# Windowed-softmax heads taken by fours in a decoder layer, with the probabilities turned by DMA

## The chip, the core and the metric

The kernel runs on one core of one Trainium2 chip. The core has TensorE (PE, matrix products, with weight loads PEld beside them), VectorE (DVE), ScalarE (ACT), GpSimd (POOL) and SyncE (SP), which here only issues DMAs. The metric is the time of one execution in microseconds; the median of three runs is compared. Lower is better.

## The reference

One decoder layer on 256 positions of width 2048, in float32, batch 1:

```python
mod = (silu(c) @ w_ada + b_ada).reshape(9, D)                 # conditioning: shifts, scales, gates
x = x + 0.5 * mod[2] * swiglu(modulate(rms_norm(x), mod[0], mod[1]), w_ffn1_gu, w_ffn1_down)
h = modulate(rms_norm(x), mod[3], mod[4])
rq, rk, rv, rg, sq, sk, sv, gl_ret, gl_swa = split(h @ w_in)  # one projection, 2048 x 13312
y_ret = (silu(rg) * group_rms(retention(rotary(rq), rotary(rk), rv))) @ w_ret_branch
y_swa = swa_with_sinks(sq, sk, sv, sinks) @ w_swa_branch
x = x + mod[5] * ((sigmoid(gl_ret) * y_ret + sigmoid(gl_swa) * y_swa) @ w_out)
x = x + 0.5 * mod[8] * swiglu(modulate(rms_norm(x), mod[6], mod[7]), w_ffn2_gu, w_ffn2_down)
return rms_norm(x)
```

The part that the change is about is `swa_with_sinks`: 32 query heads of 64 share 8 key and value heads (four each). Positions stand in two blocks of 128. A query of the first block sees keys of its own block, one of the second sees both, within a window of 128. Each head has a learned "sink" logit that joins the softmax's sum and takes no value.

## The kernel before

Nearly all work is projections. A weight tile `raw` of 4 x 128 rows by 512 columns comes by DMA (`load`, L328), is split in two halves of 1024 columns each: ACT casts a half to `wh` (L351), DVE subtracts to get the remainder `wl` (L353), in three buffers each. PE multiplies each half with both blocks of 128 positions: 12 products of 128x512, L343 (high times high), L344 (low activations), L345 (low weights). `in_chunk` makes 512 columns of the combined projection: four such tiles, so eight halves.

Other work is hung between the tiles. After each half `tick()` may advance the conditioning, `ada_pass`, a multiply-and-sum on DVE over rows of `w_ada` (L206) that share the pool of four `raw` buffers; `pace["rate"]` is the number of passes per half. After each tile `turn_step()` advances transpositions by DMA (`turn_by_dma`: ACT writes a tile's low and high 16-bit halves as two planes, SP issues a transposing DMA at L500, ACT puts the planes together at L511), and `step()` advances a list of side work, `side`: the windowed softmax, then the retention heads. Except on SP, whose order is the program's, a scheduler then orders each engine's instructions; each engine runs its own list in order.

The windowed softmax goes by pairs of heads, 16 pairs. `window_weights(pair)`: logits on PE, two heads beside each other in the array's two row halves (L1097 for the first block of queries, L1101 for the second), scaled and masked by DVE (L1105), maxima, sum and sink on DVE, four exponentials on ACT (L1136), four scalings on DVE (L1145). `window_values(pair)`, a step later: six turns of 128x128 on PE against the identity (`transpose_to`, L478), evacuated by ACT (L479), then the products with the values (L1165, L1170) and a copy into `qo` (L1177). The residual `x` stays in SBUF in `x_sb` all the while. The table `dec` of decay factors for retention is loaded by POOL when the combined projection begins.

Of the kernel before, what the change touches and what calls it, by code (L numbers as in the profile page):

```python
# [17 lines left out]
P = 128  # L18
# [59 lines left out]
def layer_kernel(  # L78
# [257 lines left out]
    def products(banks, ah, al, wh, wl, starts, ends, halves=range(NT)):  # L336
        n = ah.shape[1]
        for j in range(n):
            first, last = starts and j == 0, ends and j == n - 1
            for t in halves:  # L340
                ts = slice(t * P, (t + 1) * P)
                ps = banks[t]
                nc.tensor.matmul(ps, ah[:, j, ts], wh[:, j, :], start=first, stop=False)  # L343
                nc.tensor.matmul(ps, al[:, j, ts], wh[:, j, :], start=False, stop=False)  # L344
                nc.tensor.matmul(ps, ah[:, j, ts], wl[:, j, :], start=False, stop=last)  # L345

    def split(pool, tag, src, n, hi_engine="act"):
        k = src.shape[1]
        hi = pool.tile([P, 2, n], F32R, tag=tag + "h", name=nm(tag + "h"))[:, :k, :]
        lo = pool.tile([P, 2, n], F32R, tag=tag + "l", name=nm(tag + "l"))[:, :k, :]  # L350
        cast.append(nc.scalar.copy(hi, src).ins)  # L351
        del cast[:-1]
        nc.vector.tensor_sub(lo, src, hi.bitcast(F32))  # L353
        return hi, lo

    cast = []

    def pair_tile():
        return asp.tile([P, 2, CH], F32, tag="a", name=nm("a"))
# [725 lines left out]

    mask = small_c[:, C_MASK : C_MASK + 3 * P]

    def window_weights(pair):

        kv = pair // 2  # L1090
        lg = pair_tile()[:, :, : 3 * P]

        both = [side_bank() for _ in range(2)]
        halves = [slice(i * HD, (i + 1) * HD) for i in range(2)]
        with tc.high_priority(offset=300):
            for ps, hs in zip(both, halves):
                nc.tensor.matmul(  # L1097
                    ps[:, :P], qo[hs, pair, :P], skt[hs, kv, :P], start=True, stop=True
                )
            for ps, hs in zip(both, halves):  # L1100
                nc.tensor.matmul(  # L1101
                    ps[:, P : 3 * P], qo[hs, pair, P:], skt[hs, kv, :], start=True, stop=True
                )
        for i, ps in enumerate(both):
            nc.vector.scalar_tensor_tensor(  # L1105
                out=lg[:, i, :],
                in0=ps[:, : 3 * P],
                scalar=HD**-0.5,
                in1=mask,
                op0=ALU.mult,  # L1110
                op1=ALU.add,
            )
        mx = small(4, "mx")
        m2 = mx.rearrange("p (t i) -> p t i", t=2)
        nc.vector.tensor_reduce(out=m2[:, 0, :], in_=lg[:, :, :P], axis=AX.X, op=ALU.max)
        nc.vector.tensor_reduce(out=m2[:, 1, :], in_=lg[:, :, P:], axis=AX.X, op=ALU.max)
        sb = sink_b[:, 2 * pair : 2 * pair + 2]
        nc.vector.tensor_tensor(
            out=m2, in0=m2, in1=sb[:, None, :].broadcast_to([P, 2, 2]), op=ALU.max
        )  # L1120
        ng = small(4, "ng")
        nc.vector.tensor_scalar(out=ng, in0=mx, scalar1=-1.0, scalar2=None, op0=ALU.mult)
        se = small(4, "se")
        nc.vector.tensor_tensor(
            out=se.rearrange("p (t i) -> p t i", t=2),
            in0=ng.rearrange("p (t i) -> p t i", t=2),
            in1=sb[:, None, :].broadcast_to([P, 2, 2]),
            op=ALU.add,
        )
        nc.scalar.activation(se, se, AF.Exp)  # L1130
        sm = small(4, "sm")
        for t in range(2):
            for i in range(2):
                seg = lg[:, i, :P] if t == 0 else lg[:, i, P:]
                z = 2 * t + i
                nc.scalar.activation(  # L1136
                    seg, seg, AF.Exp, bias=ng[:, z : z + 1], accum_out=sm[:, z : z + 1]
                )
        nc.vector.tensor_add(sm, sm, se)
        nc.vector.reciprocal(sm, sm)  # L1140
        for t in range(2):
            for i in range(2):
                seg = lg[:, i, :P] if t == 0 else lg[:, i, P:]
                z = 2 * t + i
                nc.vector.tensor_scalar(  # L1145
                    out=seg, in0=seg, scalar1=sm[:, z : z + 1], scalar2=None, op0=ALU.mult
                )
        return lg

    def window_values(pair, lg):  # L1150

        kv = pair // 2
        prs = []
        for i in range(2):
            pr = a512()
            transpose_to(
                pr[:, : 3 * P], lambda j: lg[:, i, j * P : (j + 1) * P], 3, bank()
            )
            prs.append(pr)
        po = bank()  # L1160
        vs = slice(kv * HD, (kv + 1) * HD)
        halves = [slice(i * HD, (i + 1) * HD) for i in range(2)]
        with tc.high_priority(offset=300):
            for hs, pr in list(zip(halves, prs))[::-1]:
                nc.tensor.matmul(  # L1165
                    po[hs, :P], sv[:, 0, vs], pr[:, :P], start=True, stop=True
                )
            for t in range(2):
                for hs, pr in list(zip(halves, prs))[::-1]:
                    nc.tensor.matmul(  # L1170
                        po[hs, P:S],
                        sv[:, t, vs],
                        pr[:, (t + 1) * P : (t + 2) * P],
                        start=t == 0,
                        stop=t == 1,
                    )
        nc.any.tensor_copy(qo[:, pair, :], po[:, :S])  # L1177

    before = []

    def window(pair):
        lg = window_weights(pair)
        yield
        if before:
            window_values(*before.pop())
        before.append((pair, lg))
        if pair == QH // 2 - 1:
            yield
            window_values(*before.pop())
        yield  # L1190

    for ci in range(4):
        b = in_chunk(O_SQ + ci * CH)
        work = []
        for t in range(NT):
            u = t512()
            nc.any.tensor_copy(u, b[t])
            work.append(turn_by_dma(qo[:, ci * 4 : ci * 4 + 4, t * P : (t + 1) * P], u))
        pairs = range(ci * 4, ci * 4 + 4)
        soon(later(work, lambda pairs=pairs: side.extend(window(pair) for pair in pairs)))  # L1200


    qk = slot().rearrange("p (a h s) -> p a h s", a=2, h=RH)
# [34 lines left out]
    def retention(h):  # L1238
# [9 lines left out]
        dh = dec[:, h * S : (h + 1) * S]  # L1248
# [67 lines left out]
    for p in range(2):  # L1316
# [125 lines left out]
```

## Time and profile before

| | |
|---|---|
| runs | 2400.08, 2400.95, 2401.19 us; median 2400.95 |
| profiled execution | 2398.28 us, span 2396.5 us |
| granted TensorE clock | 0.999 |
| busy time of the span | PE 99%, PEld 81%, DVE 71%, ACT 54% |
| windowed softmax on PE | from 880.0 us (first logits) to 1113.8 us (last values) |
| DMA | 615.31 MB, mean 257 GB/s |

The page is one profiled execution. A row of a group gives the line, the engine, the tiles (out<-in) and sizes, the count, then busy time in us and the mean in ns, then the idle time before them and what ended it. Matmuls are pipelined, so one that lasts 0.39 us by its row may follow the last after 0.23. The timeline's first column is the start, the second the length, both in us.

### The profile page before, as it was taken

The numbers are of one execution on the slowest core, as the hardware profiler recorded it, in microseconds if no ns is written. First come the engines' busy times: TensorE is split into PE (matmuls) and PEld (weight loads), VectorE is DVE, ScalarE is ACT, GpSimd is POOL, SyncE is SP. The second block draws the span as 40 slices with busy tenths as digits, with TensorE's granted clock in tenths as the row PEclk, the third lists the DMA queues.
The fourth block names the chain that finished last, engine by engine and source line by source line (L and its number), as shares of the span: only waits on it lengthen the run. The fifth ranks groups of instructions, "written<-read, shape, count | busy, mean of one in ns | idle before, by whom it ended". The sixth has DMA issues, their size and how long they took to land. (4 is left out here: it accounts for less than half of the span.)

```text
span 2396.5 us, 28841 instructions
## 1 busy us (share of the span) xinstructions
PE 2365.2 (99%) x10662; PEld 1937.3 (81%) x10662; DVE 1696.6 (71%) x2707; ACT 1302.2 (54%) x1807; POOL 5.6 (0%) x14
## 2 busy tenths in 40 slices
PE   7999999999999999999999999999999999999998
PEld 5788888888788887778888888887888888888886
DVE  6987799788977667876666776767655555545656
ACT  6554456454456566665556554466445445454544
POOL 0000000000000000000000000000000000000000
PEclk9999999999999999999999999999999999999999
DMA  9978789998875888765679887765777777765563
GB/s 357 365 280 273 267 294 336 345 335 329 315 250 211 272 262 244 231 213 202 236 256 288 265 270 276 268 203 193 230 243 237 247 253 241 259 220 190 182 205 126
DMA packets 309614, 615.31 MB, mean 257 GB/s; under 512 B 75169, under 2 KB 75553, under 8 KB 290657
## 3 DMA queue, kind: packets, MB, share of 16 engines
q1 hardware_dynamic: 307970, 606.82, 74.6%
q0 software_dynamic: 928, 5.61, 0.6%
q8 instruction: 83, 1.36, 0.2%
q10 hardware_dynamic: 576, 1.05, 0.1%
q14 instruction: 57, 0.47, 0.1%
HBM read 595.06 MB, written 2.12 MB: 249 GB/s over the span
## 5 line engine op out<-in xcount | busy, mean ns | idle before, releaser
L353 DVE TENSOR_TENSOR wl<-raw,wh 128x1024 fp32r<-128x1024 f32 x794 | 967.2, 1224 | 553.0 <-ACT wh L351 548.8
L351 ACT CAST wh<-raw 128x1024 fp32r<-128x1024 f32 x794 | 835.1, 1053 | 932.3 <-PE pa L344 903.2
L343 PE MATMUL pa<-wh,hh 128*128 128x512 f32 x2192 | 856.2, 392 | 2.9 <-ACT wh L351 2.9
L344 PE MATMUL pa<-wh,hl 128*128 128x512 f32 x2192 | 855.7, 391 | 0.3 <-DVE hl L600 0.3
L345 PE MATMUL pa<-wl,hh 128*128 128x512 f32 x2192 | 783.6, 391 | 1.1 <-DVE wl L353 0.9
L343 PEld LDWEIGHTS pa<-wh,hh 128*128 128x128 f32 x2192 | 411.8, 188 | 89.6 <-ACT wh L351 4.4
L344 PEld LDWEIGHTS pa<-wh,hl 128*128 128x128 f32 x2192 | 412.0, 188 | 88.3 <-issue 3.0
L345 PEld LDWEIGHTS pa<-wl,hh 128*128 128x128 f32 x2192 | 409.6, 188 | 89.2 <-DVE wl L353 2.8
L344 PE MATMUL pa<-wh,a 128*128 128x512 f32 x944 | 365.2, 389 | 0.0
L343 PE MATMUL pa<-wh,a 128*128 128x512 f32 x944 | 349.8, 390 | 1.8 <-DVE t L606 1.4
L345 PE MATMUL pa<-wl,a 128*128 128x512 f32 x944 | 348.9, 390 | 1.4 <-DVE wl L353 1.4
L206 DVE CUSTOM_DVE_ANT_0 raw<-raw,cact 128x512 f32<-128x512 f32 (+1 forms) x296 | 189.9, 696 | 46.8 <-DMA raw<-in_w_ada_dram 40.0
L343 PEld LDWEIGHTS pa<-wh,a 128*128 128x128 f32 x944 | 177.3, 188 | 40.0 <-DVE t L606 2.2
L345 PEld LDWEIGHTS pa<-wl,a 128*128 128x128 f32 x944 | 177.0, 188 | 39.6 <-DVE wl L353 3.0
L344 PEld LDWEIGHTS pa<-wh,a 128*128 128x128 f32 x944 | 177.2, 188 | 36.5 <-DVE a L386 0.2
L206 DVE CUSTOM_DVE_ANT_0 slot<-slot,cact 128x512 f32<-128x512 f32 (+1 forms) x216 | 170.2, 838 | 8.6 <-DMA slot<-in_w_ada_dram 8.6
L511 ACT COPY slot<-back 128x512 uint16<-128x512 uint16 x124 | 82.7, 766 | 0.0
L386 DVE TENSOR_TENSOR a<-slot,a 128x512 fp32r<-128x512 f32 x118 | 80.9, 687 | 1.3 <-ACT a L385 1.3
L385 ACT CAST a<-slot 128x512 fp32r<-128x512 f32 x118 | 72.7, 617 | 0.9 <-DVE t L670 0.9
L495 ACT COPY flat<-t 128x512 uint16<-128x512 uint16 x112 | 63.6, 617 | 5.3 <-DVE t L1229 4.9
L206 DVE DVE_READ_ACCUMULATOR2_ANT sums<- 128x1 f32 x512 | 43.4, 85 | 0.0
L998 DVE TENSOR_TENSOR slot<-slot,pa 128x512 f32<-128x512 f32 x48 | 32.0, 686 | 3.8 <-PE pa L345 3.7
(206 smaller groups left out, 1177.4 us busy)
## 6 DMA issues: line engine op xcount, KB each, us to landing
raw<-in_w_ffn_gu_dram SPq DMA_DIRECT2D x160, 1024.0 KB, 5.4
raw<-in_w_in_dram SPq DMA_DIRECT2D x104, 1024.0 KB, 5.6
raw<-in_w_ffn_down_dram SPq DMA_DIRECT2D x88, 1024.0 KB, 5.2
raw<-in_w_ada_dram SPq DMA_DIRECT2D x73, 1024.0 KB, 5.1
slot<-in_w_ada_dram SPq DMA_DIRECT2D x67, 1024.0 KB, 7.4
raw<-in_w_ffn_gu_dram SPq DMA_DIRECT2D x32, 512.0 KB, 5.4
raw<-in_w_swa_branch_dram SPq DMA_DIRECT2D x16, 1024.0 KB, 5.4
raw<-in_w_ret_branch_dram SPq DMA_DIRECT2D x16, 1024.0 KB, 5.3
```

What stands on the lines that cost most here:

```text
L206: nc.vector.tensor_tensor_reduce(out=w[:, at], in0=w[:, at], in1=cact[:, at], scale=1.0, scalar=0.0, op0=ALU.mult, op1=ALU.add, accum_out= ...
L343: nc.tensor.matmul(ps, ah[:, j, ts], wh[:, j, :], start=first, stop=False)
L344: nc.tensor.matmul(ps, al[:, j, ts], wh[:, j, :], start=False, stop=False)
L345: nc.tensor.matmul(ps, ah[:, j, ts], wl[:, j, :], start=False, stop=last)
L351: cast.append(nc.scalar.copy(hi, src).ins)
L353: nc.vector.tensor_sub(lo, src, hi.bitcast(F32))
L385: nc.scalar.copy(hi, v)
L386: nc.vector.tensor_sub(lo, v, hi.bitcast(F32))
L495: nc.scalar.copy(planes[:, i, :], words(src)[:, :, i])
L511: nc.scalar.copy(into[:, :, :, i], held["turned"][:, i])
L998: nc.vector.tensor_add(p, p, b)
```

## The change

The windowed softmax goes by four heads (a "quad", those that share one key and value head), eight times. Four parts:

- *Logits and values in bursts.* `quad_weights(g)` issues eight logit products in one run, into two `side_bank`s and two `bank`s, directly behind the newest projection. `quad_values(g)` issues six value products of 256 columns (two heads in one).
- *Probabilities turned by DMA.* No PE turns: `quad_apart` writes the probabilities as 16-bit planes on ACT, `quad_turn` issues two transposing DMAs on SP, `quad_together` puts the planes together on DVE. Scaling is one two-input operation per block with a broadcast factor.
- *x in DRAM.* `x_sb` is written to `x_d` by POOL after the first feed-forward stage, its place in SBUF holds logits and turned probabilities (`soft`), and it is read back ahead of the output projection. The planes lie in the buffer `row`, where `dec` was; `dec` is now loaded after the last quad's planes are read.
- *Conditioning.* 0.95 passes per half (before 192/262), 0.25 while the softmax runs, 0.95 after.

```diff
-    dec = one.tile([P, D], F32, tag="row", name="dec")
-    nc.gpsimd.dma_start(dec, consts[:, C_DEC:])
-    set_pace([(7, 2, None), (6, None, None), (5, None, 1.0)], 262, raw_row, 2)
+    x_d = tc.dram_tile([NT, P, D], F32, name="x_d")
+    for t in range(NT):
+        nc.gpsimd.dma_start(x_d[t], x_sb[:, t, :])
+    soft = one.tile([P, NT * D], F32, tag="x", name="soft")
+    planes_of = one.tile([P, D], F32, tag="row", name="planes_of")
+    RATE_SOFT, RATE_AFTER = 0.25, 0.95
+    set_pace([(7, 2, None), (6, None, None), (5, None, 1.0)], 192 / 0.95, raw_row, 2)
...
+    def quad_weights(g):
...
+        with tc.issue_after(newest[-1]), tc.high_priority(offset=300):
+            for ps, qs, n in ((late, slice(P, S), S), (early_q, slice(0, P), P)):
+                for a in range(2):
+                    for i, hs in enumerate(halves):
+                        nc.tensor.matmul(
+                            ps[i][:, a * n : (a + 1) * n],
+                            qo[hs, 2 * g + a, qs], skt[hs, g, :n], start=True, stop=True,
+                        )
...
+        for t, of_t in enumerate(parts_of):
+            for i in range(HQ):
+                z = t * HQ + i
                 nc.scalar.activation(
-                    seg, seg, AF.Exp, bias=ng[:, z : z + 1], accum_out=sm[:, z : z + 1]
+                    of_t[:, i, :], of_t[:, i, :], AF.Exp,
+                    bias=ng[:, z : z + 1], accum_out=sm[:, z : z + 1],
                 )
         nc.vector.tensor_add(sm, sm, se)
         nc.vector.reciprocal(sm, sm)
...
+        for t, of_t in enumerate(parts_of):
+            nc.vector.tensor_tensor(
+                out=of_t, in0=of_t,
+                in1=sm[:, t * HQ : (t + 1) * HQ][:, :, None].broadcast_to(
+                    [P, HQ, of_t.shape[2]]
+                ),
+                op=ALU.mult,
+            )
+
+    def quad_apart():
+
+        with tc.issue_after(cast[-1]):
+            for a in range(2):
+                src = logits[:, 2 * a : 2 * a + 2, :].rearrange("p h n -> p (h n)")
+                for i in range(2):
+                    nc.scalar.copy(planes[:, a, i, :], words(src)[:, :, i])
+
+    def quad_turn():
...
+        for a in range(2):
+            nc.sync.dma_start_transpose(
+                turned[a].rearrange("p (k n) -> p k n", n=P),
+                planes[:, a].rearrange("p i n -> p (i n)"),
+            )
+        return turned
+
+    def quad_together(turned):
...
+            with tc.issue_after(low[-1]):
+                for i in range(2):
+                    nc.vector.tensor_copy(
+                        words(into)[:, :, i], turned[a][:, i * 2 * W3 : (i + 1) * 2 * W3]
+                    )
+
+    def quad_values(g):
...
+        with tc.issue_after(newest[-1]), tc.high_priority(offset=300):
+            for t, blk, tv in ((0, 0, 0), (1, 1, 0), (1, 2, 1)):
+                for i in (1, 0):
                     nc.tensor.matmul(
+                        p4[halves[i], :, t, :], sv[:, tv, vs], heads[:, :, i, blk, :],
+                        start=blk < 2, stop=blk != 1,
                     )
...
+    def softmax_heads():
...
+        for at in range(4 * (QUADS + 1) + 2):
+            g, part = divmod(at, 4)
+            if part == 0 and g < QUADS:
+                quad_weights(g)
+            if part == 1 and g >= 2:
+                quad_values(g - 2)
+            if part == 2 and g >= 1:
+                turned[g - 1] = quad_turn()
+            if part == 2 and g < QUADS:
+                quad_apart()
+            if part == 3 and g >= 1:
+                quad_together(turned.pop(g - 1))
+                if g == QUADS:
+                    dec.append(one.tile([P, D], F32, tag="row", name="dec"))
+                    nc.gpsimd.dma_start(dec[0], consts[:, C_DEC:])
             yield
+        pace["rate"] = RATE_AFTER
...
     gate_load(gate, 5)
+    x_sb = one.tile([P, NT, D], F32, tag="x", name="x_sb")
+    for t in range(NT):
+        nc.gpsimd.dma_start(x_sb[:, t, :], x_d[t])
```

`newest`, `cast` and `low` hold the last projection, cast and subtraction that the program has issued; `issue_after` only sets an order on that engine, no wait. Lines behind the change shift: L345 becomes L346, L351 L356, L353 L358, L500 L506, L511 L517.

On PE, in the middle of the softmax (the query projections), before: `pd` are logit banks, `ps` a value bank, `pa` the projections.

```order
L343 MATMUL pa_7087<-wh_7107,hh_4112 128x512
L1097 MATMUL pd_7260<-slot_6195,slot_6353 128x128
L1097 MATMUL pd_7261<-slot_6195,slot_6353 128x128
L1165 MATMUL ps_7073<-t_7067,slot_6195 64x128
L1165 MATMUL ps_7073<-t_7061,slot_6195 64x128
L1170 MATMUL ps_7073<-t_7067,slot_6195 64x128
L1170 MATMUL ps_7073<-t_7061,slot_6195 64x128
L1170 MATMUL ps_7073<-t_7067,slot_6195 64x128
L1170 MATMUL ps_7073<-t_7061,slot_6195 64x128
L1101 MATMUL pd_7260<-slot_6195,slot_6353 128x256
L1101 MATMUL pd_7261<-slot_6195,slot_6353 128x256
L344 MATMUL pa_7087<-wh_7107,hl_4113 128x512
```

The same place now, first the logits of the fourth quad (L1117), then, three halves later, the values of the second (L1201):

```order
L346 MATMUL pa_7506<-wl_7527,hh_4112 128x512
L1117 MATMUL pd_7549<-slot_6198,slot_6360 128x256
L1117 MATMUL pd_7550<-slot_6198,slot_6360 128x256
L1117 MATMUL pd_7549<-slot_6198,slot_6360 128x256
L1117 MATMUL pd_7550<-slot_6198,slot_6360 128x256
L1117 MATMUL ps_7551<-slot_6198,slot_6360 128x128
L1117 MATMUL ps_7552<-slot_6198,slot_6360 128x128
L1117 MATMUL ps_7551<-slot_6198,slot_6360 128x128
L1117 MATMUL ps_7552<-slot_6198,slot_6360 128x128
L343 MATMUL pa_7505<-wh_7589,hh_4112 128x512
```
```order
L344 MATMUL pa_7505<-wh_7655,hl_4113 128x512
L343 MATMUL pa_7506<-wh_7655,hh_4112 128x512
L1201 MATMUL ps_7626<-soft,slot_6198 64x2x128 x6
L346 MATMUL pa_7505<-wl_7656,hh_4112 128x512
L344 MATMUL pa_7506<-wh_7655,hl_4113 128x512
```

Eight logit products stand together where four did, with values apart from them and no turns between.

On DVE, around the scaling of a softmax, before: `a` holds a pair's logits, `sm` its sums, `mx` maxima, `wl` weight remainders.

```order
L1139 TENSOR_TENSOR sm_7694<-sm_7694,se_7691 128x4
L353 TENSOR_TENSOR wl_7787<-raw_7767,wh_7786 128x1024
L1105 SCALAR_TENSOR_TENSOR a_7805<-pd_7806,small_c 128x384
L1105 SCALAR_TENSOR_TENSOR a_7805<-pd_7807,small_c 128x384
L353 TENSOR_TENSOR wl_7837<-raw_7834,wh_7836 128x1024
L1140 RECIPROCAL sm_7694<-sm_7694 128x4
L1115 TENSOR_REDUCE mx_7814<-a_7805 128x2
L1116 TENSOR_REDUCE mx_7814<-a_7805 128x2
L353 TENSOR_TENSOR wl_7854<-raw_7834,wh_7853 128x1024
L1145 TENSOR_SCALAR a_7676<-a_7676,sm_7694 128x128 x2
L1145 TENSOR_SCALAR a_7676<-a_7676,sm_7694 128x256 x2
```

And now, in the fourth quad: L1140 is the negated maximum, on which the exponentials wait; L1150 waits for them.

```order
L1139 TENSOR_TENSOR mx_7565<-mx_7565,sink_b 128x8
L358 TENSOR_TENSOR wl_7700<-raw_7681,wh_7699 128x1024
L1140 TENSOR_SCALAR ng_7566<-mx_7565 128x8
L1188 COPY soft<-a_7673 128x768 x2
L1188 COPY soft<-a_7674 128x768
L1141 TENSOR_TENSOR se_7567<-ng_7566,sink_b 128x8
L1188 COPY soft<-a_7674 128x768
L1150 TENSOR_TENSOR sm_7568<-sm_7568,se_7567 128x8
L1151 RECIPROCAL sm_7568<-sm_7568 128x8
L1153 TENSOR_TENSOR soft<-soft,sm_7568 128x4x128
L1153 TENSOR_TENSOR soft<-soft,sm_7568 128x4x256
L358 TENSOR_TENSOR wl_7738<-raw_7735,wh_7737 128x1024
```

Between the two subtractions (L358) now stand the whole end of the softmax and the putting together of the third quad's planes (L1188).

On SP, in the same rounds, before, with conditioning rows (L201) and turning DMAs of the rotary projections (L500):

```order
L328 DMA raw_7494<-in_w_in_dram 128x4x512
L201 DMA raw_7528<-in_w_ada_dram 128x2048
L500 DMA_TRANSPOSE back_7531<-flat_7199 128x8x128
L328 DMA raw_7562<-in_w_in_dram 128x4x512
L328 DMA raw_7634<-in_w_in_dram 128x4x512
L328 DMA raw_7705<-in_w_in_dram 128x4x512
L201 DMA raw_7723<-in_w_ada_dram 128x2048
```

And now:

```order
L328 DMA raw_7634<-in_w_in_dram 128x4x512
L201 DMA raw_7652<-in_w_ada_dram 128x2048
L506 DMA_TRANSPOSE back_7671<-flat_7397 128x8x128
L1176 DMA_TRANSPOSE a_7673<-planes_of 128x12x128
L1176 DMA_TRANSPOSE a_7674<-planes_of 128x12x128
L328 DMA raw_7681<-in_w_in_dram 128x4x512
L328 DMA raw_7735<-in_w_in_dram 128x4x512
L328 DMA raw_7815<-in_w_in_dram 128x4x512
```

Two turning DMAs of 12 blocks stand ahead of a weight tile, and conditioning rows are fewer.

More of the change, by code (lines that the diff above doesn't have):

```diff
@@ L1086, in layer_kernel @@
     mask = small_c[:, C_MASK : C_MASK + 3 * P]
[L1088 to L1098, printed above, removed]
-                )
[L1100 to L1121, printed above, removed]
-        nc.vector.tensor_scalar(out=ng, in0=mx, scalar1=-1.0, scalar2=None, op0=ALU.mult)
[L1123 to L1129, printed above, removed]
-        nc.scalar.activation(se, se, AF.Exp)
[L1131 to L1135, printed above, removed]
@@ L1140, in window_weights @@
         nc.vector.reciprocal(sm, sm)
[L1141 to L1157, printed above, removed]
-            )
-            prs.append(pr)
-        po = bank()
[L1161 to L1175, printed above, removed]
-                    )
-        nc.any.tensor_copy(qo[:, pair, :], po[:, :S])
@@ L1179, in layer_kernel @@
[L1179 to L1187, printed above, removed]
+        for t, of_t in enumerate(parts_of):
+            nc.vector.tensor_tensor(
[4 more added lines that the diff above has]
+                op=ALU.mult,
+            )
@@ new lines, in quad_apart @@
+    def quad_apart():
[5 more added lines that the diff above has]
+    def quad_turn():
+        turned = [pair_tile() for _ in range(2)]
+        turned = [
+            t.rearrange("p i n -> p (i n)").bitcast(U16)[:, : 4 * W3] for t in turned
+        ]
+        for a in range(2):
[4 more added lines that the diff above has]
+        return turned
@@ L1198, in layer_kernel, with asking @@
             work.append(turn_by_dma(qo[:, ci * 4 : ci * 4 + 4, t * P : (t + 1) * P], u))
-        pairs = range(ci * 4, ci * 4 + 4)
-        soon(later(work, lambda pairs=pairs: side.extend(window(pair) for pair in pairs)))
+        def asking(ci=ci):
+            asked.add(ci)
+            if ci == 0:
+                pace["rate"] = RATE_SOFT
+                side.append(softmax_heads())
+        soon(later(work, asking))
     qk = slot().rearrange("p (a h s) -> p a h s", a=2, h=RH)
```

54 lines of the change are left out of this document (48 added, 6 removed).

## The prediction

> **What bounds the kernel now.** I read the page first: its busy time by engine and its chain.
>
> ```profile
> span 2396.5 us, 28841 instructions
> PE 2365.2 (99%) x10662; PEld 1937.3 (81%) x10662; DVE 1696.6 (71%) x2707; ACT 1302.2 (54%) x1807; POOL 5.6 (0%) x14
> ...
> PE 42%; DVE 1%; issue 0%; ACT 0%; DVEq 0%
> ```
>
> TensorE (PE) is busy for all but 31 us of the span, and in the chain it has 42% of the span against 1% for all others. Work taken off PE shortens the kernel directly, as long as PE is still fed. So I asked next for PE's groups with shapes apart, in the stretch from the first logits to the last values of the attention (879 to 1115 us):
>
> ```profile
> L343 PE MATMUL pa<-wh,hh 128*128 128x512 f32 x275 | 109.0, 396 | 0.0
> L344 PE MATMUL pa<-wh,hl 128*128 128x512 f32 x275 | 108.4, 394 | 0.0
> L345 PE MATMUL pa<-wl,hh 128*128 128x512 f32 x276 | 106.7, 397 | 0.0
> L478 PE MATMUL ps<-small_c,a 128*128 128x128 f32 x96 | 14.7, 274 | 0.0
> L1101 PE MATMUL pd<-slot,slot 64*128 64x256 f32 x64 | 13.4, 387 | 0.0
> L1097 PE MATMUL pd<-slot,slot 64*128 64x128 f32 x64 | 11.2, 322 | 0.0
> L1170 PE MATMUL ps<-t,slot 128*64 128x128 f32 x128 | 9.7, 273 | 0.0
> L1165 PE MATMUL ps<-t,slot 128*64 128x128 f32 x64 | 7.0, 298 | 0.0
> L1241 PE MATMUL pd<-slot 128*128 128x256 f32 x2 | 0.6, 377 | 0.0
> L1244 PE MATMUL pd<-slot 128*128 128x128 f32 x2 | 0.4, 274 | 0.0
> ```
>
> The idle column is zero throughout: nothing starves PE here. Matmuls overlap, so a duration is not a price; the price is the distance between starts. The timeline of PE gives it:
>
> ```profile
> 975.57 0.39 PE L344 MATMUL pa<-wh,hl 128*128 128x512 f32 x1
> 975.88 0.44 PE L1165 MATMUL ps<-t,slot 128*64 128x128 f32 x4
> 976.15 0.61 PE L1170 MATMUL ps<-t,slot 128*64 128x128 f32 x8
> 976.69 0.72 PE L345 MATMUL pa<-wl,hh 128*128 128x512 f32 x2
> 977.25 0.40 PE L343 MATMUL pa<-wh,hh 128*128 128x512 f32 x1
> 977.49 0.40 PE L344 MATMUL pa<-wh,hl 128*128 128x512 f32 x1
> 977.82 0.49 PE L1097 MATMUL pd<-slot,slot 64*128 64x128 f32 x4
> 978.14 0.60 PE L1101 MATMUL pd<-slot,slot 64*128 64x256 f32 x4
> 978.67 0.51 PE L345 MATMUL pa<-wl,hh 128*128 128x512 f32 x1
> 979.01 0.39 PE L343 MATMUL pa<-wh,hh 128*128 128x512 f32 x1
> ...
> 984.68 0.39 PE L344 MATMUL pa<-wh,hl 128*128 128x512 f32 x1
> ```
>
> From 979.01 to 984.68 stand 25 intervals between projection matmuls: 0.227 us each. The stretch holds 275 + 275 + 276 = 826 of them, 187.5 us of its 236; the first retention scores (L1241, L1244) are under 1 us. So attention costs PE **47.8 us**. Its parts: the values of one pair took 977.25 - 975.57 less three projections, 1.00 us; the logits of one pair 979.01 - 977.49 less two, 1.07 us.
>
> **PE after the change.** The 96 turns of L478 go. The other multiplications move as many columns as before, in 16 bursts (eight of logits, eight of values, four heads each) instead of up to 32. Two heads run side by side, so a burst is a row of passes of two instructions: a pair's logits are two passes of 128 columns and two of 256, its values six of 128. With a fixed part f for the way in and out, a for a pass of 128 columns and 2a for one of 256, both come to f + 6a, and both took about 1.03. The split is open. The L1170 row has four passes from 976.15 to 976.69, 0.54 with the way back: a is at most 0.135, and f then 0.22. A quarter of a projection's 0.227 is the least that 128 columns can take: a = 0.057, f = 0.69. I take a = 0.11, f = 0.37, near the first end, since it is read from the passes themselves. Four heads are f + 12a, logits and values alike: 1.7 us, 16 times is 27, so PE is spared **21 us**. The two ends give 29.4 and 21.9, spared 18 and 26.
>
> **What feeds PE.** Each half of a weight tile needs a ScalarE (ACT) cast and a VectorE (DVE) subtraction before 12 projections (2.72 us):
>
> ```profile
> L351 ACT CAST wh<-raw 128x1024 fp32r<-128x1024 f32 x69 | 72.3, 1049 | 50.8 <-PE pa L344 45.9 <-PE pa L345 1.8 <-ACT wh L351 1.7
> ```
> ```profile
> L353 DVE TENSOR_TENSOR wl<-raw,wh 128x1024 fp32r<-128x1024 f32 x794 | 967.2, 1224 | 553.0 <-ACT wh L351 548.8
> ...
> L511 ACT COPY slot<-back 128x512 uint16<-128x512 uint16 x124 | 82.7, 766 | 0.0
> L386 DVE TENSOR_TENSOR a<-slot,a 128x512 fp32r<-128x512 f32 x118 | 80.9, 687 | 1.3 <-ACT a L385 1.3
> L1378 DVE TENSOR_SCALAR t<-t,rs 128x512 f32<-128x512 f32 x6 | 2.6, 482 | 0.1
> ```
> ```profile
> 979.22 0.16 DVE L1124 TENSOR_TENSOR se<-ng,sink_b 128x4 f32<-128x4 f32 x1
> 981.21 0.16 DVE L1139 TENSOR_TENSOR sm<-sm,se 128x4 f32<-128x4 f32 x1 [1.83 <-ACT a L1136]
> 981.41 0.18 DVE L1140 RECIPROCAL sm<-sm 128x4 f32<-128x4 f32 x1
> 981.62 1.01 DVE L1145 TENSOR_SCALAR a<-a,sm 128x128 f32<-128x128 f32 x4
> ```
>
> The casts mostly wait for PE to give a buffer back, 45.9 us of 50.8: they run the full three buffers ahead. The lead of a subtraction is then two halves less its own chain, 5.44 - 1.05 - 1.22 = 3.2 us.
>
> The chain of four heads is longer than that of two. In the row order, DVE issues the negated maximum, then must wait for all exponentials, with later subtractions queued behind. For two heads that hole was 981.21 - 979.22 = 2.0 us; with eight exponentials 4.0. Sum and reciprocal take 0.4. The scaling becomes two two-input operations of 512 and 1024 elements: 0.69 (L386) + 1.22 (L353) = 1.9. Putting the turned planes together is new on DVE: four 16-bit copies of 768. By the nearest row of the same engine with one input (L1378, 482 ns for 512) one takes 0.72, by ACT's 16-bit copy (L511) 1.15; I take 0.72, 2.9 in all. With two subtractions (2.4) DVE needs 11.6 us to deliver two halves, against 5.44 + 3.2 and the 1.7 us of a value burst between: 10.3. That is 1.3 short. By the order, in about half of the eight rounds the copies stand inside the wait for the exponentials and nothing is short. So four rounds at 1.3: **5 us** of new PE stall. Bounds: none, or eight rounds at the dearer copy (+1.7) with no value burst in the window: 8 x 4.7 = 37 us.
>
> Here the Trainium skill (VectorE: DVE Perf Modes, The perf-mode tier table) prices the copy lower: one-input fp32 work inside SBUF at 1227 ns for 2048 elements, by proportion an estimate of 0.46 us for 768. By it 10.6 us stand against 10.3, the stall is 1 us and the sum -20; no row before the change has this copy on DVE.
>
> **Edits costed at nothing, and their covers.**
>
> ```profile
> L500 SPq DMA_TRANSPOSE back<-flat x62: 1237/1272/8145, 335.6 to 2119.9; - x62
> ...
> DMA to landing us min/median/max: 3.2/6.3/13.2
> ```
> ```profile
> raw<-in_w_in_dram SPq DMA_DIRECT2D x104, 1024.0 KB, 5.6
> ```
> ```profile
> SPq L328 <- DVE wl L353: 1013.3, 245, 7.2
> ```
> ```profile
> L206 DVE CUSTOM_DVE_ANT_0 raw<-raw,cact 128x512 f32<-128x512 f32 x292 | 185.0, 688 | 40.6 <-DMA raw<-in_w_ada_dram 40.0
> ```
> ```profile
> 1300.00:1340.00 40.00, 40.00 (x178) 33.09 (x177) 27.29 (x41) 26.06 (x34) 0.00 (x0) 1.00 0.95 297
> ...
> 1380.00:1420.00 40.00, 40.00 (x178) 33.15 (x177) 31.25 (x50) 22.35 (x28) 0.00 (x0) 1.00 0.76 253
> ```
>
> - *Sixteen transfers that turn*, half as large again as those of L500, stand on SyncE (SP) ahead of a weight load. Two issues of 1.27 us are hidden: weight loads wait on average 1013.3 / 245 = 4.1 us for a buffer.
> - *ACT* gains four plane copies of 768 per four heads (1.15 each by L511), and loses four evacuations. The casts' wait for PE covers it; they stand after two casts.
> - *Conditioning* falls from 192/262 = 0.73 to 0.25 steps per half in the attention and rises to 0.95 outside. That moves (0.73 - 0.25) x 76 halves = 37 passes, 25 us of DVE by L206, to stages where DVE is busy up to 31.25 of 40 us (the two-column products of the branches) and PE waited for nothing. Its loads rise there too, but 297 GB/s stood in the trace with PE at 40.00 of 40.
> - *x in DRAM*: 2 MB out right after the first feed-forward stage and 2 MB back, queued on GpSimd (POOL) ahead of the second gate, hundreds of us before anything reads it.
> - *The decay table* is loaded only after the last planes are read, shortly before retention. If it is late, DVE waits in order with subtractions behind it: 0 to about the 6.3 us of a transfer. I take 0, since eight subtractions stand between.
>
> **Sum.** Profiled execution 2398.28 us (span 2396.5): -21 + 5 = -16, so 2382.3. The median of the three runs is 2400.95, 2.7 above the profiled one; I predict the median: **2385**.
>
> **Rivals.**
>
> 1. *The cover holds everywhere*, with no new stall: -21, 2380. For: casts wait for PE in 45.9 of 50.8 us. Against: the lead of 3.2 us is shorter than the new hole.
> 2. *Bursts save little*: each pair pays its own way in and out as now, 16 x 2.07 = 33.1, so only 14.7 us are spared, less 5: 2391. For: the array is still switched around each pair of heads. Against: the row order holds the eight instructions together.
> 3. *The softmax chain by fours starves PE*, the slower side: 37 - 21 = +16, 2417. Its place is the subtraction behind the scaling; it decides from 21/8 = 2.6 us of stall per round on. Against it: the copies often stand inside the exponentials' wait.
> 4. *The turning transfers hold SP.* One issue of L500 took 8145 ns; two such are 16.3 us against 2.5. A weight buffer comes round every 4 x 5.44 = 21.8 us, of which its transfer (5.6) and two halves' work (2.72 + 2.3) leave 11. Then 13.8 - 11 = 2.8 late per round, 22 in all: +6, 2407. The Trainium skill (VectorE: DVE Perf Modes, The three transpose paths) speaks for it: it gives 390 ns for a 128x128 turn on TensorE against 1309 ns by DMA and says to use TensorE where PSUM will do. The trace agrees that a turn by transfer lands late (6.3 us), not that anyone waits for it.
> 5. *Conditioning does not fit its new place*: the 25 us of DVE all lie on the path: 25 - 16 = +9, 2410.
>
> **Chances.** Forecast 0.48; cover holds 0.25; little saved 0.08; starving 0.10; SP 0.05; conditioning 0.04. Measurements of this kernel tell 0.2% (4.8 us) from no change. The first two are faster, rival 2 at half, the last three slower: faster 0.77, same 0.04, slower 0.19. The range goes from the full saving at its upper end (-26: 2375) up to past the nearest slower rival (2408); beyond it lie the starving and the conditioning case, 0.14.
>
> **What would show it.** Right: 192 fewer PE matmul records (96 turns, and the values in half as many records), 16 bursts of about 1.7 us, PE idle in the attention stretch of some 5 us ended by DVE's subtraction, the stretch shorter by about 16. Wrong: PE waits ended by DVE or ACT of over 2.6 us a round there; weight casts that wait for loads behind the turning transfers; DVE idle on the decay table; PE idle between attention and output projection that was not there.

## The result, and the profile after

The changed kernel takes 2385.91 us (median of four runs, 2383.35 to 2390.51) against 2400.66 (four runs, 2400.08 to 2401.19): ratio 0.9941, 95% interval 0.9923 to 0.9958. The prediction was 2385.0, and faster. Its profiled execution took 2383.35 us, 14.9 less than the one of before. The sum was near, but its second term, the stall, came from another place than the one that was forecast.

The page of the changed kernel, its span and the engines' busy time:

```profile
span 2381.5 us, 28418 instructions
...
PE 2346.1 (99%) x10470; PEld 1922.2 (81%) x10470; DVE 1703.2 (72%) x2635; ACT 1309.8 (55%) x1792; POOL 7.7 (0%) x18
```

10662 - 10470 = 192 PE records are gone. PE's idle time is 2381.5 - 2346.1 = 35.4 us, 4.1 more than the 31.3 of before. The groups of PE between 879 and 1115 us (busy us, mean ns, then idle time before):

```profile
L343 PE MATMUL pa<-wh,hh 128*128 128x512 f32 x302 | 119.2, 395 | 0.5 <-ACT wh L356 0.5
L344 PE MATMUL pa<-wh,hl 128*128 128x512 f32 x302 | 117.6, 389 | 0.0
L346 PE MATMUL pa<-wl,hh 128*128 128x512 f32 x302 | 110.8, 394 | 0.0
L1201 PE MATMUL ps<-soft,slot 128*64 128x256 f32 x96 | 12.1, 388 | 0.0
L1117 PE MATMUL pd<-slot,slot 64*128 64x256 f32 x64 | 9.1, 402 | 0.0
L1117 PE MATMUL ps<-slot,slot 64*128 64x128 f32 x64 | 4.9, 271 | 0.0
```

906 projections stand where 826 stood, and PE never stood idle for VectorE: the last column is zero for L346, where the prediction put 5 us. (The 0.5 us of L343 is a wait for a ScalarE cast.) A burst is priced by the starts of the projections around it. From the last one before it to the second one behind it, less two steps of 0.227 us, it costs 1.707 us for logits and 1.645 for values. The second one is taken because the first step behind a burst is itself longer, 0.335 us. 8 x (1.707 + 1.645) = 26.8 us, against 47.6 for the attention before. That is the whole gain, 20.8 us. The new copies, in the trace of the tile `soft` (ns shortest/median/longest):

```profile
L1167 ACT COPY planes_of<-soft x32: 822/829/836, 895.3 to 1071.3; 128x768 uint16<-128x768 uint16 x32
L1188 DVE COPY soft<-a x32: 592/606/625, 921.1 to 1094.7; 128x768 uint16<-128x768 uint16 x32
```

What was lost again shows in the windows, first of the kernel before, then of the changed one (length, then busy time of PE, PEld, DVE, ACT and POOL with counts, granted clock, DMA share, GB/s):

```profile
880.00:1140.00 260.00, 260.00 (x1354) 205.15 (x1354) 201.94 (x464) 166.85 (x343) 0.00 (x0) 1.00 0.68 222
1140.00:1640.00 500.00, 497.79 (x2199) 410.24 (x2198) 349.69 (x540) 279.77 (x361) 1.05 (x2) 1.00 0.76 258
```
```profile
880.00:1140.00 260.00, 259.52 (x1248) 206.82 (x1247) 200.68 (x336) 184.16 (x338) 1.59 (x3) 1.00 0.83 246
1140.00:1640.00 500.00, 494.02 (x2175) 405.30 (x2174) 363.32 (x602) 276.37 (x359) 1.05 (x2) 1.00 0.79 268
```

Behind the attention PE is idle for 6.0 us instead of 2.2, VectorE is busy 13.6 us more (its conditioning passes, L206, 81.5 us instead of 66.1). The waits in that stretch (total, times, longest), before and after:

```profile
DVE raw L206 <- DMA raw<-in_w_ada_dram: 11.5, 10, 2.8
PEld pa L345 <- DVE wl L353: 3.5, 5, 0.9
```
```profile
DVE raw L206 <- DMA raw<-in_w_ada_dram: 25.5, 20, 3.1
PEld pa L346 <- DVE wl L358: 8.4, 9, 1.6
PE pa L346 <- DVE wl L358: 4.9, 7, 1.2
```

VectorE waits longer for conditioning rows, with subtractions queued behind it, and PE for the subtractions. In the timelines three stalls of PE, at 1297, 1308 and 1485 us, come 3 to 5 us after such waits of VectorE (3.07, 1.49 and 1.46 us).

A busy PE hides small losses, since a record (0.39 us) outlasts its step (0.227). For all runs below the starts of the projections were therefore compared: the **lengthening** is the sum of what the steps from one projection to the next exceed 0.227 us, bursts taken out. All kernels have the same 9984 projections.

| kernel | lengthening 880-1140 us | 1140-1640 us | median us |
|---|---|---|---|
| before | 5.7 | 5.9 | 2400.66 |
| changed | 4.7 | 11.2 | 2385.91 |
| e10, changed again | 4.7 | 10.8 | 2386.52 |
| e1, old pacing | 21.0 | 6.1 | 2399.27 |
| e2, pacing between | 10.4 | 9.7 | 2391.38 |
| e8, old pacing, rows earlier | 24.7 | 7.6 | 2402.18 |
| e5, together copies twice | 13.2 | 15.4 | 2398.23 |
| e3, turns on PE | 5.7 | 12.3 | 2399.63 |
| e4, pairs, new pacing | 5.6 | 11.7 | 2404.27 |
| e6, rows three steps ahead | 5.0 | 18.8 | 2389.80 |
| e6, rows four steps ahead | 4.2 | 10.6 | 2387.14 |
| e9, rows in buffers of their own | 4.4 | 6.4 | 2382.66 |

(The kernel before took 2401.25, 2401.13 and 2400.98 us beside the three groups of runs, so medians compare across them.)

The first step behind each burst, some 0.1 us too long, is still in these columns. In the attention this makes 5.0 of the 5.7 us before (49 bursts, turns included) and 3.1 of the 4.7 us now (24 bursts). Steps of over 0.25 us that follow no burst, the real stalls, add up to 0 before, 1.0 in the changed kernel, 18.0 in e1, 7.0 in e2, 10.1 in e5 and 0 in e3. Behind the attention the same count gives 4.2 before, 9.5 changed and 4.3 in e9, so the differences there stand.

### The profile page after: what moved, and what is told of

Read it like the earlier page. It is cut to its first block, busy times and chain, and to the rows that moved or that the text cites. A ratio compares the mean times of both kernels' runs of the same rounds, so it can differ in the third digit from the quotient of the medians.

```text
span 2381.5 us, 28418 instructions
## 1 busy us (share of the span) xinstructions
PE 2346.1 (99%) x10470; PEld 1922.2 (81%) x10470; DVE 1703.2 (72%) x2635; ACT 1309.8 (55%) x1792; POOL 7.7 (0%) x18
## 5 line engine op out<-in xcount | busy, mean ns | idle before, releaser
L358 DVE TENSOR_TENSOR wl<-raw,wh 128x1024 fp32r<-128x1024 f32 x794 | 964.7, 1222 | 526.4 <-ACT wh L356 524.2
L356 ACT CAST wh<-raw 128x1024 fp32r<-128x1024 f32 x794 | 834.1, 1053 | 921.5 <-PE pa L344 881.8
L343 PE MATMUL pa<-wh,hh 128*128 128x512 f32 x2192 | 855.0, 391 | 3.3 <-ACT wh L356 3.3
L346 PE MATMUL pa<-wl,hh 128*128 128x512 f32 x2192 | 778.0, 392 | 0.3 <-DVE wl L358 0.2
L343 PEld LDWEIGHTS pa<-wh,hh 128*128 128x128 f32 x2192 | 411.6, 188 | 93.1 <-ACT wh L356 5.3
L346 PEld LDWEIGHTS pa<-wl,hh 128*128 128x128 f32 x2192 | 410.1, 188 | 88.0 <-DVE wl L358 2.0
L346 PE MATMUL pa<-wl,a 128*128 128x512 f32 x944 | 349.4, 390 | 4.6 <-DVE wl L358 4.6
L343 PE MATMUL pa<-wh,a 128*128 128x512 f32 x944 | 349.4, 390 | 1.9 <-DVE t L612 1.4
L206 DVE CUSTOM_DVE_ANT_0 raw<-raw,cact 128x512 f32<-128x512 f32 (+1 forms) x296 | 189.8, 694 | 44.2 <-DMA raw<-in_w_ada_dram 37.8
L346 PEld LDWEIGHTS pa<-wl,a 128*128 128x128 f32 x944 | 176.6, 188 | 44.3 <-DVE wl L358 7.9
L343 PEld LDWEIGHTS pa<-wh,a 128*128 128x128 f32 x944 | 177.1, 188 | 40.1 <-DVE t L612 2.2
L206 DVE CUSTOM_DVE_ANT_0 slot<-slot,cact 128x512 f32<-128x512 f32 (+1 forms) x216 | 169.9, 834 | 15.9 <-DMA slot<-in_w_ada_dram 15.8
L517 ACT COPY slot<-back 128x512 uint16<-128x512 uint16 x124 | 82.8, 767 | 0.0
L206 DVE DVE_READ_ACCUMULATOR2_ANT sums<- 128x1 f32 x512 | 42.0, 82 | 0.0
```

The source lines that it names most:

```text
L206: nc.vector.tensor_tensor_reduce(out=w[:, at], in0=w[:, at], in1=cact[:, at], scale=1.0, scalar=0.0, op0=ALU.mult, op1=ALU.add, accum_out= ...
L358: low.append(nc.vector.tensor_sub(lo, src, hi.bitcast(F32)).ins)
L517: nc.scalar.copy(into[:, :, :, i], held["turned"][:, i])
```

## Experiments

**e1: the old pacing.** The first question was why no stall came in the attention and one came behind it.

```diff
-    RATE_SOFT, RATE_AFTER = 0.25, 0.95
-    set_pace([(7, 2, None), (6, None, None), (5, None, 1.0)], 192 / 0.95, raw_row, 2)
+    RATE_SOFT, RATE_AFTER = 192 / 262, 192 / 262
+    set_pace([(7, 2, None), (6, None, None), (5, None, 1.0)], 262, raw_row, 2)
```

> The changed kernel with the old even pacing of the conditioning (0.73 steps per half everywhere, instead of 0.25 in the attention and 0.95 outside); all else as changed. Theory A: the changed kernel's PE idle of 5.9 us between 1140 and 1620 us (0.84 before) is the conditioning that was moved there, so here it falls back to about 1 us; some 37 passes (25 us of VectorE) return to the attention, VectorE rises there from 187 to about 212 us of 236, and if the softmax still has cover the time is 2386 - 5 = about 2381. Theory A with the prediction's own stall term (a hole of 11.6 us against a cover of 10.3): the hole opens now, 5 us or more of PE idle in the attention, about 2386 or more. Rival B: the idle time behind the attention has another cause (x on its way through DRAM, turning transfers, another order of loads): it stays at about 5 us, and the time is 2386 or more.

2399.27 us (11 runs; ratio to before 0.999, 0.9981 to 0.9999): nearly all the gain is gone. Theory A with the prediction's stall term holds, and at three times its size. The windows:

```profile
880.00:1140.00 260.00, 247.99 (x1173) 193.60 (x1172) 214.28 (x401) 175.63 (x329) 1.58 (x3) 0.99 0.86 261
1140.00:1640.00 500.00, 497.93 (x2200) 410.35 (x2198) 349.23 (x541) 278.74 (x359) 1.05 (x2) 1.00 0.77 259
```

Behind the attention PE idles 2.1 us as before the change; in it 12.0. The lengthening there is 21.0 us, 16.3 more than with the new pacing (by the times at which the same projections start, e1 falls back 18.8 us against the changed kernel in the attention). One such hole, in VectorE's timeline (start, length, in brackets the idle time before):

```profile
895.25 0.17 DVE L1150 TENSOR_TENSOR sm<-sm,se 128x8 f32<-128x8 f32 x1 [3.58 <-ACT soft L1146]
895.45 0.20 DVE L1151 RECIPROCAL sm<-sm 128x8 f32<-128x8 f32 x1
896.83 0.69 DVE L206 CUSTOM_DVE_ANT_0 raw<-raw,cact 128x512 f32<-128x512 f32 x1 [1.18 <-DMA raw<-in_w_ada_dram]
...
899.28 1.82 DVE L1153 TENSOR_TENSOR soft<-soft,sm 128x512 f32<-128x512 f32 x2
901.02 2.35 DVE L358 TENSOR_TENSOR wl<-raw,wh 128x1024 fp32r<-128x1024 f32 x2
```

No subtraction starts until 901.02, while VectorE waits for the exponentials (3.6 us) and for a late conditioning row (1.2), makes four passes over it and does the scalings. That is the prediction's hole, with 3.6 us of conditioning (895.65 to 899.28) inside it. On PE at the same moment:

```profile
898.91 0.40 PE L344 MATMUL pa<-wh,hl 128*128 128x512 f32 x1
902.29 1.22 PE L346 MATMUL pa<-wl,hh 128*128 128x512 f32 x2 [2.98 <-DVE wl L358]
903.32 0.63 PE L343 MATMUL pa<-wh,hh 128*128 128x512 f32 x1
...
907.15 0.63 PE L344 MATMUL pa<-wh,hl 128*128 128x512 f32 x1
907.58 0.90 PE L346 MATMUL pa<-wl,hh 128*128 128x512 f32 x2
908.32 0.39 PE L343 MATMUL pa<-wh,hh 128*128 128x512 f32 x1
```

**e2: pacing between the two.**

```diff
-    RATE_SOFT, RATE_AFTER = 0.25, 0.95
-    set_pace([(7, 2, None), (6, None, None), (5, None, 1.0)], 192 / 0.95, raw_row, 2)
+    RATE_SOFT, RATE_AFTER = 0.45, 0.86
+    set_pace([(7, 2, None), (6, None, None), (5, None, 1.0)], 192 / 0.85, raw_row, 2)
```

> The changed kernel with the conditioning paced between the two: 0.85 steps per half ahead of the attention, 0.45 in it, 0.86 behind it. Theory A (the moved conditioning is what is lost behind the attention): PE idle between 1140 and 1620 us falls from 5.9 to some 2 us, no stall in the attention, about 2382. Rival B: the idle stays, 2386.

2391.38 us (ratio 0.9958, 0.9944 to 0.9971): slower than the changed kernel, against the expectation of 2382. Behind the attention the lengthening falls only from 11.2 to 9.7; in it, where none was expected, it more than doubles, from 4.7 to 10.4. So the cover ends somewhere between a pace of 0.25 and one of 0.45.

**e4: the new pacing on the kernel before.**

```diff
-    set_pace([(7, 2, None), (6, None, None), (5, None, 1.0)], 262, raw_row, 2)
+    set_pace([(7, 2, None), (6, None, None), (5, None, 1.0)], 192 / 0.95, raw_row, 2)
...
+            pace["rate"] = 0.95
...
+            if ci == 0:
+                pace["rate"] = 0.25
```

> The kernel before (pairs of heads, turns on PE) with the new pacing alone: 0.95 steps per half ahead of and behind the attention, 0.25 in it. Theory A: no PE work is saved and the five us of idle time appear behind the attention as in the changed kernel: 2401 + 5 = about 2406, PE matmul records as before (10662). Rival C: pacing by itself brings part of the gain: 2396 or less. If the idle time behind the attention comes only with the heads by fours (rival B): about 2401.

2404.27 us (ratio 1.0014, 1.0005 to 1.0023): slower, so pacing by itself is no gain (rival C falls). Behind the attention the lengthening is 11.7 us against 5.9 without the heads by fours (rival B falls): the loss there belongs to the pacing. That only 3.0 of these 6 us show in the medians, and 4.4 between the profiled executions, agrees with the attention: by the times of the same projections it ran 1.8 us quicker, since 13 pairs of bursts instead of 9 fell together.

**e3: turns on PE.**

```diff
-            if part == 2 and g >= 1:
-                turned[g - 1] = quad_turn()
...
-                quad_apart()
+                for h in range(HQ):
+                    transpose_to(
+                        turned_p[:, h].rearrange("p b q -> p (b q)"),
+                        lambda j, h=h: logits[:, h, j * P : (j + 1) * P], 3,
+                    )
...
-                quad_together(turned.pop(g - 1))
```

> The changed kernel, but with the probabilities turned on TensorE (12 turns of 128x128 per four heads, evacuated from PSUM), without plane copies on ScalarE, turning transfers and together copies on VectorE. By the prediction (PE work is time, a turn costs 0.11 us): 96 x 0.11 = 10.5 us slower than the changed kernel, about 2396. Rival: the transfers and copies cost as much elsewhere (SP's issues, DMA load, VectorE), so that turning on PE is no more than 3 us slower, or faster: 2386 to 2389 or less. The Trainium skill (VectorE: DVE Perf Modes, The three transpose paths) advises TensorE for such turns, which speaks for the rival.

(With no transfer to wait for, a quad's values also come one round earlier than in the changed kernel.)

2399.63 us, 13.1 more than the changed kernel (2386.52): the rival falls. The groups of PE between 879 and 1140 us:

```profile
L484 PE MATMUL ps<-small_c,soft 128*128 128x128 f32 x96 | 14.2, 272 | 0.0
...
L1113 PE MATMUL pd<-slot,slot 64*128 64x256 f32 x64 | 9.1, 402 | 0.0
L1113 PE MATMUL ps<-slot,slot 64*128 64x128 f32 x64 | 5.5, 291 | 0.0
```

Nothing waits here either. 96 turns at 0.112 us are 10.7. The rest is a by-product: six of the eight bursts of logits broke in two (the turns use the same PSUM banks, which is the likely reason). Half a burst costs 1.059 us, a whole one 1.708, so 2 x 1.059 - 1.708 = 0.41 us is what each way in and out costs, and six more of them 2.5 us. 10.7 + 2.5 = 13.2.

**e5: VectorE's work alone.** e1 had brought back two things, VectorE's passes and their transfers. Here only VectorE gets more work.

```diff
-                for i in range(2):
+                for i in (0, 1, 0, 1):
                     nc.vector.tensor_copy(
```

> The changed kernel with the four copies that put the turned planes together done twice per four heads (the second time into the same place): 4 x 0.6 = 2.4 us more on VectorE per round, 19 us in the attention, and no more transfers. It separates VectorE's load from the conditioning's transfers, which the even pacing brought back together (that run lost 18 us in the attention). Theory D (VectorE's work itself has used up the cover there): each round loses up to 2.4 us, 10 to 19 in all, 2396 to 2405. Theory E (what the even pacing lost was VectorE waiting for late conditioning rows, with subtractions queued behind; its work alone still has cover): 0 to 4 us, 2386 to 2390.

2398.23 us (ratio 0.9993, 0.9981 to 1.0004), 11.7 more than the changed kernel: theory D. The copies added take 32 x 0.488 = 15.6 us of VectorE (their records last 0.604 us, but one starts 0.488 us after the other). Of this the lengthening in the attention shows 13.2 - 4.7 = 8.5. Another 4.2 us of the loss lie behind the attention (15.4 against 11.2), where the edit adds no work: there a single stall at 1365 us, after VectorE had waited 2.6 us for a row, costs 4.0 with the slow products that follow it. Waits between 880 and 1140 us:

```profile
DVE sm L1150 <- ACT soft L1146: 16.1, 6, 3.6
PEld pa L346 <- DVE wl L358: 8.8, 7, 2.1
PE pa L346 <- DVE wl L358: 5.8, 6, 1.7
...
DVE raw L206 <- DMA raw<-in_w_ada_dram: 3.9, 2, 2.4
```

VectorE waits for rows no longer than in the changed kernel (3.8 us), and PE still stalls. e1 had lost twice as much (16.3 us) with less work added (214.28 - 200.68 = 13.6 us in its window); there VectorE also waited 17.6 us for rows. That the rest of e1's loss is these waits is argued, not shown.

**e8 and e6: rows asked for earlier.** Theory E, that the losses are late rows, was tried three times: the old pacing with rows four steps ahead instead of two (e8, in its call of `set_pace`), and the changed kernel with three or four behind the attention (e6).

```diff
         pace["rate"] = RATE_AFTER
+        pace["ahead"] = 4
```

> The changed kernel with the old even pacing (0.73 steps per half everywhere) and its rows asked for four steps ahead instead of two. With two steps ahead the even pacing lost 18 us in the attention against the changed kernel, with VectorE waiting 17.6 us there for rows. Theory E (late rows, with subtractions queued behind): most of it comes back, 12 us or more, about 2387 or less. Theory D (VectorE's work has used up the cover): the loss stays, 2395 or more.

> The changed kernel, with the conditioning rows behind the attention asked for three steps ahead instead of two. Between 1140 and 1640 us VectorE waited 25.5 us (20 times) for these rows in the changed kernel and 11.5 (10 times) in the one before, with subtractions queued behind; PE's steps between projections were there 11.2 us longer than 0.227 each, against 5.9. Theory E (late rows are what is lost behind the attention): the wait falls to 12 us or less, PE's lengthening to 6 to 8, the time by 3 to 5 us to about 2381 to 2383. Theory F (the transfers are simply too many at 0.95, or VectorE too busy): the wait moves to the weight tiles, the time stays at 2386 or rises.

> As the run with three steps ahead, with four. Theory E: no wait for rows left, 2380 to 2382. Theory F, stronger here, since each row then holds one of the buffers that the weight tiles use for a step longer: casts wait for weight tiles, 2386 or more.

2402.18, 2389.80 and 2387.14 us: no gain in any. What falls is the remedy of theory E. Whether late rows are the cause these runs can't say, since the rows came no earlier: VectorE's wait for rows in the attention of e8 was 16.2 us (17.6 in e1), and behind the attention in e6 it was not 12 us or less but (three, then four steps):

```profile
DVE raw L206 <- DMA raw<-in_w_ada_dram: 53.1, 24, 4.3
PEld pa L346 <- DVE wl L358: 13.6, 14, 2.5
```
```profile
DVE raw L206 <- DMA raw<-in_w_ada_dram: 31.6, 21, 5.0
PEld pa L346 <- DVE wl L358: 4.8, 6, 2.0
```

Asking earlier did not shorten the wait. The likely reason is that a row must take its turn in the ring of four buffers that the weight tiles go through, which e9 tests. (The profiled execution with three steps was a long one of its kernel, 2392.73 us; the median is 2389.80.)

**e9: rows in buffers of their own**, with e10, the changed kernel once more, as its base. The place of x is free from the last softmax to the reload of x.

```diff
+    own = []
+
+    def row_at():
+        if not own:
+            return raw_row()
+        own.append(own.pop(0))
+        return own[-1]
+
...
-    set_pace([(7, 2, None), (6, None, None), (5, None, 1.0)], 192 / 0.95, raw_row, 2)
+    set_pace([(7, 2, None), (6, None, None), (5, None, 1.0)], 192 / 0.95, row_at, 2)
...
         pace["rate"] = RATE_AFTER
+        both = one.tile([P, NT * D], F32, tag="x", name="own")
+        own.extend([both[:, :D], both[:, D:]])
+        pace["ahead"] = AQ
```

> The changed kernel, where the conditioning behind the attention keeps its rows in two buffers of its own (in the place that the softmax has left and that x comes back to later) instead of in the ring that the weight tiles use, each asked for four steps ahead. The same rows at the same 0.95 steps per half. Asking earlier within the shared ring had not shortened VectorE's wait for rows (25.5 us between 1140 and 1640 us with two steps, 53.1 with three, 31.6 with four). Theory G (the rows are late because the ring gives them a buffer late): the wait falls to 12 us or less, PE's lengthening there from 11.2 to about 6, the time by some 5 us, 2381. Theory F (the transfers themselves are too many at 0.95, or VectorE too busy): the wait stays at 20 us or more, or casts wait for weight tiles instead; 2385 to 2390.

> The changed kernel once more, on the chip of the runs with it, as their base: 2386, within 2383 to 2391.

2382.66 us (five runs, 2379.92 to 2384.59; ratio 0.9927, 0.9913 to 0.9941) against 2386.52 (five, 2384.15 to 2389.17; ratio 0.9943, 0.9930 to 0.9955). It is the fastest version of this study, 3.9 us below the changed kernel by the medians; the intervals against before overlap a little. The lengthening behind the attention is 6.4 us, as theory G wanted. The windows and waits there:

```profile
1140.00:1640.00 500.00, 497.20 (x2197) 409.35 (x2196) 365.21 (x601) 277.68 (x363) 2.11 (x4) 1.00 0.78 270
```
```profile
DVE own L206 <- DMA own<-in_w_ada_dram: 19.9, 20, 2.4
PEld pa L346 <- DVE wl L358: 4.1, 6, 1.2
PE pa L346 <- DVE wl L358: 2.0, 3, 0.8
```

The same rate (268 GB/s in the changed kernel) and the same VectorE work now fit, so neither was too much (theory F falls in the time). But VectorE's wait for rows, 19.9 us, did not fall to the 12 that theory G gave: it is 25.5 in the changed kernel and 23.4 in e10, and its longest fell from 3.1 and 2.9 to 2.4. Whether the shorter waits or the buffers set free for weight tiles brought the gain stays open.

## Why the prediction was right, point by point

- *PE work is time; bursts cost 0.37 us plus 0.11 a pass; 27 us in all, 21 spared.* Right in each figure: 26.8 and 20.8 us; by e3's halves 0.41 us for the way in and out, and (1.708 - 0.41) / 12 = 0.108 a pass.
- *Four rounds at 1.3 us, 5 us of new stall in the attention.* This step failed: the real stalls there are 1.0 us. Of these 0.8 (at 895 us) is PE waiting for a ScalarE cast that stood behind the eight exponentials of the first quad, and only 0.2 (at 1051 us) is a wait for VectorE. The second quad's round in VectorE's timeline shows why:

```profile
913.83 0.17 DVE L1140 TENSOR_SCALAR ng<-mx 128x8 f32<-128x8 f32 x1
914.14 1.22 DVE L358 TENSOR_TENSOR wl<-raw,wh 128x1024 fp32r<-128x1024 f32 x1
917.79 0.17 DVE L1150 TENSOR_TENSOR sm<-sm,se 128x8 f32<-128x8 f32 x1 [2.42 <-ACT soft L1146]
918.23 1.83 DVE L1153 TENSOR_TENSOR soft<-soft,sm 128x512 f32<-128x512 f32 x2
919.97 1.22 DVE L358 TENSOR_TENSOR wl<-raw,wh 128x1024 fp32r<-128x1024 f32 x1
921.11 2.06 DVE L1188 COPY soft<-a 128x768 uint16<-128x768 uint16 x4
923.05 1.21 DVE L358 TENSOR_TENSOR wl<-raw,wh 128x1024 fp32r<-128x1024 f32 x1
```

  The chain was sized too long. The exponentials took 4.0 us (913.83 to 917.79), as forecast. But records overlap on VectorE as they do on PE: a together copy lasts 0.606 us and the next one starts after 0.488, four of them take 1.94 (921.11 to 923.05) and not 2.9, and the scalings take 1.74 and not 1.9. By starts the chain is 4.0 + 0.4 + 1.7 + 2.0 + 2.4 = 10.5 us (wait, sum and reciprocal, scalings, copies, two subtractions) against the 10.3 of cover, where the prediction had 11.6. By starts the copy is also near the 0.46 that the prediction estimated from the Trainium skill (VectorE: DVE Perf Modes, The perf-mode tier table); by its record it is not.

  The chain was also not in one piece. In six of the eight rounds a subtraction stands inside the wait for the exponentials, as at 914.14, and in the five rounds whose copies come after the scaling at least one stands between them, as at 919.97. (The order of the fourth quad, shown ahead of the prediction, is one of only two in which copies stand inside the wait, not one of half.) The idea of a hole in VectorE's deliveries with little cover was right: e5, with 2 us more per round, loses 8.5 us, and e1 and e2 show that the lower pacing keeps the hole closed. The prediction had priced the pacing by what it loads on other stages and not by what it relieves.
- *Conditioning fits behind the attention, at nothing.* This step failed too, by 11.2 - 5.9 = 5.3 us; the argument was that 297 GB/s had stood with PE busy in 40.00 of 40. Bandwidth was not the limit: e9 moves 270 GB/s at nearly no loss. What counted was the ring that rows and weight tiles share, since with rows out of it the loss is gone; which of the two had waited for the other stays open. This was rival 5's place, at a fifth of its price.
- *The sum, -21 + 5 = -16.* Measured -14.9 between the profiled executions: -20.8 on PE, some 1.0 of stalls in the attention and 5.3 behind it give -14.5. The 5 us were the right size by luck: they came from a term that the prediction had put at nothing.
- *Edits at nothing.* The turning transfers held no cast that PE noticed: one cast in the attention waited 4.0 us for a weight tile (until 1039 us), and PE did not pause there. ScalarE's plane copies took 0.829 us each and hid. x through DRAM and the decay table stand in no wait of PE between 880 and 1640 us; VectorE waited 1.6 us for the table.
- *Rival 1* (cover holds) was true of the attention. *Rival 2* (33.1 us of bursts) is refuted by 26.8. *Rival 3* (starving) is what e1, at the old pacing, turned the change into, at 2399 us in a milder form than the 2417 forecast. *Rival 4* (turning transfers hold SP) is refuted, and with it, for this kernel, the rule of the Trainium skill to turn on TensorE where the result may go to PSUM (VectorE: DVE Perf Modes, Rules for kernel authors): that way costs 13.1 us, since PE is the bound and the transfers are covered.

## What to carry to other kernels

Where one engine is 99% busy, count its instructions and the cost of entering and leaving each special mode: that part of the forecast held to 0.2 us. Price other engines by the distance between starts as well, not by the length of a record. Before calling added work on another engine hidden, look at what else that engine does in the same stretch: the change stands on some 14 us of VectorE work having been taken out of its way, and without that it gains 2 us instead of 15. A load that queues for buffers that others turn over was not cured here by asking earlier (e6, e8); buffers of its own did it (e9).

## What was not expected of the hardware

A stall can cost more than itself. After the idle 2.98 us in e1 (rows above) the products followed each other at 0.427 us instead of 0.227, twelve of them, until 908.0 us: 2.4 us more. The granted clock in the windows of e1:

```profile
900.00:902.00 2.00, 0.00 (x0) 0.00 (x0) 2.00 (x2) 0.82 (x2) 0.00 (x0) 0.84 0.57 128
902.00:904.00 2.00, 1.71 (x4) 1.42 (x5) 2.00 (x3) 2.00 (x4) 0.00 (x0) 0.50 1.02 385
...
910.00:912.00 2.00, 2.00 (x11) 1.65 (x10) 1.22 (x1) 2.00 (x4) 0.00 (x0) 1.00 1.04 382
```

Another stall of the same run, 3.41 us at 985 us, left the clock at 1.00; in e5 one of 2.12 us at 1365 us was followed by seven products at 0.427. So length alone does not decide. The Trainium skill (TensorE: Matmul & The Clock Gate, Part 1) says that the clock halves after an idle window of about 3.4 us, counted by windows that run freely. The halving agrees (0.50). That the longest of these stalls left the clock whole would fit windows that run freely, but no run here shows the windows. And here 2.12 us of idle time were enough.
